# Moving the squares of x, their sum and three small loads from the first matrix product to the second

## The chip, the core and the metric

The kernel runs on one core of one Trainium2 chip. A core has five engines with queues of their own: TensorE (PE in the profile; its weight loads are listed apart as PEld), VectorE (DVE), ScalarE (ACT), GpSimd (POOL) and SyncE (SP), which here only issues DMAs. Each engine works through its own queue in order and waits on semaphores for the others. The metric is the device time of one execution in microseconds (us), lower is better.

## The reference

One layer of a decoder trunk in float32: 256 tokens, width 2048. Shortened to what matters here:

```python
h = rms_norm(x, norm_mix_pre)                 # x * rsqrt(mean(x*x) + eps) * gain
c_q, c_kv, k_r, q_s, k_s, v_s, gates = split(h @ w_in)
o_a = mla_attention(...)                      # from c_q, c_kv, k_r
o_b = swa_attention(q_s, k_s, v_s, swa_sinks, rel_bias_table)   # window of 128, bias by distance, sinks
merged = sigmoid(gA) * (o_a @ w_o_mla) + sigmoid(gB) * (o_b @ w_o_swa)
x = x + rms_norm(merged @ w_out, norm_mix_post)
x = x + rms_norm(conv_ffn(rms_norm(x, norm_ffn_pre)), norm_ffn_post)
```

The part that the change touches is the first norm, x * rsqrt(mean(x*x) + eps), and the start of the window branch (q_s, k_s, v_s).

## The kernel before

**Products.** All matrix products are done in parts: each float32 operand is split into a rounded high part and the rest, and three matmuls (high by high, high by low, low by high) make one product (`mm3`, L147 to L149). The activations are split into `ahl` (L207 on ScalarE, L208 on VectorE). Weights come in chunks of 512 KB, 128 x 1024: SyncE issues the load into one of three buffers `raw` (L119), ScalarE rounds it to `whi` (L121), VectorE takes the difference `wlo` (L122), and a ring of five `whi`/`wlo` buffers lies between these and TensorE. A `raw` buffer is given back when `wlo` is made, so the load of a chunk waits for the `wlo` of the chunk three before it.

**Products in order.** `gemm` runs over 16 blocks of 128 rows of the weights, for two blocks of 128 tokens. With 512 columns a chunk holds two blocks of rows, 12 matmuls. The first product makes the keys and values of the window branch (`acc_kv`). In it, chunks are 1, 1, 1, 1, 1, 1, 2, 2, 2, 2, 2 blocks (`XCUT`), because x itself is loaded and split beside the weights (`x_cols`, called once for each chunk). The second to fifth products make the queries of the window branch, 512 columns each; the accumulators of the third take the two PSUM buffers that `acc_kv` had.

**The norm.** The products take x times the gain, without the factor of the norm, which is applied to their results. `x_square(i)` squares part i of x on ScalarE (L246 for the first two parts, L249 after) and adds it to `sq_sum` on VectorE (L250). Of the eleven parts, 0 to 5 are squared in the first product and 6 to 10 in the second. `x_norm` adds the two halves of `sq_sum` (L280), sums over partitions with four small matmuls into `ssx` (L283), and makes the factor `r1` in some twelve small steps on VectorE.

**Steps.** Outside of the first product, work is hung on a list of steps. `at(t, f)` registers f for step t; `gemm` calls `tick()` after each chunk, which runs what is registered for that step. So step t of the second product comes behind its chunk t, counted from 0, and steps 8 to 15 belong to the third product. Before, step 3 has `swa_begin` (the norm) and `x_strip`; step 4 `swa_kv`, which reads `acc_kv` out, multiplied by `r1` (`kd` L315 and L316, `vs` L318); steps 5 to 8 have `swa_v` and `swa_k`, which flip values and keys on TensorE (`vr` L324, `kt` L331) and split the results (L204, L205). The window branch follows: transposed queries (`xp`, L369) at steps 9 and 10, the first scores (L399, L401) at step 10 with their read-out on VectorE (L403 to L405), which adds `bias`.

**The biases.** `x_strip` makes a strip of the biases with two matmuls from `relx` and `sel` (L275), copies it (L276) and writes it to memory from GpSimd's queue (L277). From there GpSimd loads `bias` for each pair of heads (L391, L392), for the first one at step 9. `sink` is used after the scores (L410).

**Order.** In the first product the order on VectorE, ScalarE and SyncE is the order of the program (`manual_schedule`, closed by `head.close()`). Behind it a scheduler sets the order on each engine, by priority and by its own estimate of when inputs are ready; the priority follows the order in which the program registers the work, `high_priority(300)` around the norm and the read-out of `acc_kv` raises theirs, and `keep_in_program_order` holds an instruction behind those that stand before it on its engine.

Of the kernel before, what the change touches and what calls it, by code (L numbers as in the profile page):

```python
# [16 lines left out]
ALU = mybir.AluOpType  # L17
AX = mybir.AxisListType

P = 128  # L20
# [21 lines left out]
def trunk_layer(ctx, tc, x, x_cols_in, conv_cols_in, g_mix_post, g_ffn_post, w_in, w_q, w_kv,  # L42
                sinks, rel, wo_a, wo_b, w_out, w_up, w_down, rope_tab, strip_sel, out):
    nc = tc.nc
    vec, act, pe, pool = nc.vector, nc.scalar, nc.tensor, nc.gpsimd
# [13 lines left out]
    def sb(pl, shape, name, dt=F32, tag=None, bufs=None):  # L59
        return pl.tile(shape, dt, name=name, tag=tag or name, **({"bufs": bufs} if bufs else {}))  # L60
# [30 lines left out]
    sink = sb(base, [P, SH], "sink")  # L91
# [37 lines left out]
    def at(t, *fs):  # L129
        steps[max(t, now[0])].extend(fs)  # L130
# [48 lines left out]
    def rsqrt(v, n, name, pl):  # L179
        y = sb(pl, [P, n], f"{name}_y")  # L180
        t = sb(pl, [P, n], f"{name}_t")
        u = sb(pl, [P, n], f"{name}_u")
        vec.tensor_scalar(y.bitcast(I32), v.bitcast(I32), -0.5, float(0x5F3759DF), op0=ALU.mult, op1=ALU.add)
        def vyy():
            if n == 1:
                vec.scalar_tensor_tensor(t, v, y[:, 0:1], y, op0=ALU.mult, op1=ALU.mult)
            else:
                vec.tensor_tensor(t, y, y, op=ALU.mult)
                vec.tensor_tensor(t, t, v, op=ALU.mult)


        vyy()
        vec.tensor_scalar(t, t, -0.5, 1.5, op0=ALU.mult, op1=ALU.add)
        vec.tensor_tensor(y, y, t, op=ALU.mult)
        vyy()
        vec.tensor_scalar(u, t, 0.375, -1.25, op0=ALU.mult, op1=ALU.add)
        vec.tensor_tensor(u, u, t, op=ALU.mult)
        vec.scalar_tensor_tensor(y, u, 1.875, y, op0=ALU.add, op1=ALU.mult)
        return y

    def split_to(hi, lo, src, scale=None):

        if scale is None:
            act.copy(hi, src)  # L204
            vec.tensor_tensor(lo, src, hi.bitcast(F32), op=ALU.subtract)  # L205
        else:
            act.activation(hi, src, AF.Copy, scale=scale)  # L207
            vec.scalar_tensor_tensor(lo, src, scale, hi.bitcast(F32), op0=ALU.mult, op1=ALU.subtract)  # L208
# [8 lines left out]
    def load_xt(i):  # L217
        k, ke = XCUT[i], XCUT[i + 1]
        if i == 0:
            nc.sync.dma_start(gx, x_cols_in[:, 0:38 + 256])  # L220
        else:
            nc.sync.dma_start(xr[i - 1], x_cols_in[:, 38 + k * 256:38 + ke * 256].rearrange("p (k n) -> p k n", n=256))
# [10 lines left out]
    sq_sum = sb(p0, [P, 2, 256], "sq_sum")  # L233
# [6 lines left out]
    def x_square(i):  # L240

        k, n = XCUT[i], XCUT[i + 1] - XCUT[i]
        src = xr[i - 1] if i else gx[:, 38:].unsqueeze(1)
        dst = sq_sum[:, k % 2:k % 2 + n, :]
        if k < 2:
            act.activation(dst, src, AF.Square)  # L246
        else:
            sq = sb(p0, [P, n, 256], f"sq{i}", tag="sq", bufs=2)
            act.activation(sq, src, AF.Square)  # L249
            vec.tensor_tensor(dst, dst, sq, op=ALU.add)  # L250

    def x_cols(k, ke):
        i = XCUT.index(k)
        if i > 0:
            load_xt(i)
        if i == X_AT:
            nc.sync.dma_start(relx[0:32, :], rel)
            nc.sync.dma_start(sel, strip_sel)
            nc.sync.dma_start(sink, sinks.partition_broadcast(P))
        if i > 7:  # L260
            x_square(2 * i - 16)
            x_square(2 * i - 15)
        for j in range(k, ke):
            src = xr[i - 1][:, j - k, :] if i else gx[:, 38:]
            split_to(XH(j), XL(j), src, gx[:, j:j + 1])
# [3 lines left out]
    relx = sb(lpool, [33, SH], "relx")  # L269
    pool.memset(relx[32:33, :], 1.0)  # L270
    sel = sb(lpool, [33, 384], "sel")

    def x_strip():
        pp = pss.tile([P, 512], F32, name="pstrip", tag="s")
        pe.matmul(pp[0:SH, 0:384], relx, sel, start=True, stop=True)  # L275
        vec.tensor_copy(sel[0:SH, :], pp[0:SH, 0:384])  # L276
        pool.dma_start(strip, sel[0:SH, :])  # L277

    def x_norm():
        vec.tensor_tensor(sq_sum[:, 0, :], sq_sum[:, 0, :], sq_sum[:, 1, :], op=ALU.add)  # L280
        pv_ = pss.tile([P, 512], F32, name="ssx", tag="s")
        for t in range(NT):
            pe.matmul(pv_[:, t:t + 1], sq_sum[:, 0, t * P:(t + 1) * P], ones, start=True, stop=True)  # L283
        vec.tensor_scalar(v1, pv_[:, 0:NT], 1.0 / D, EPS, op0=ALU.mult, op1=ALU.add)
        r = rsqrt(v1, NT, "r1", base)
        vec.tensor_scalar(r1s, r, 0.125, None, op0=ALU.mult)
        vec.tensor_scalar(rh, r, 0.5, None, op0=ALU.mult)
        return r

    warm_up(WARM[1])  # L290
    acc_kv, _ = gemm(XH, XL, w_in, 0, KT, C_KS, 512, pre=x_cols, extra={i: (None, p0, 4) for i in range(4)})
    pool.tensor_copy(gmat, gx[:, 0:38])
    head.close()
# [5 lines left out]
    def swa_begin():  # L299
        nonlocal es1, p1, r1  # L300
        with tc.high_priority(300):
            r1 = x_norm()
        es0.close()
        es1, p1 = open_pool("p1")
        kx.extend(sb(p1, [P, 2, 384], f"kx{g}", F32R) for g in range(4))
        vx.extend(sb(p1, [P, 4, 2, 64], f"vx{t}", F32R) for t in range(NT))

    def swa_kv(t):
        with tc.high_priority(300):
            swa_evac(t)  # L310

    def swa_evac(t):
        kk = sb(p1, [P, 4, 2, 64], f"kd{t}", tag="pth", bufs=2)
        a3 = acc_kv[t].rearrange("p (a b) -> p a b", b=64)
        act.activation(kk[:, :, 0, :], a3[:, 0:4, :], AF.Copy, scale=r1[:, t:t + 1])  # L315
        vec.tensor_scalar(kk[:, :, 1, :], a3[:, 0:4, :], r1[:, t:t + 1], None, op0=ALU.mult)  # L316
        v_ = sb(p1, [P, 256], f"vs{t}", tag="p", bufs=3)
        act.activation(v_, acc_kv[t][:, 256:512], AF.Copy, scale=r1[:, t:t + 1])  # L318
        kd.append(kk)
        vs.append(v_)  # L320

    def swa_v(t):
        pv_ = pss.tile([P, 512], F32, name=f"vr{t}", tag="s")
        pe.matmul(pv_[:, 0:256], flip, vs[t], start=True, stop=True)  # L324
        o = pv_[:, 0:256].rearrange("p (a b) -> p a b", b=64)
        split_to(vx[t][:, :, 0, :], vx[t][:, :, 1, :], o)

    def swa_k(g):
        pt = pst.tile([P, 512], F32, name=f"kt{g}", tag="t")
        for j, t in enumerate((1, 0, 1)):  # L330
            pe.matmul(pt[:, j * P:(j + 1) * P], kd[t][:, g, :, :].rearrange("p a b -> p (a b)"), flip, start=True, stop=True)  # L331
        split_to(kx[g][:, 1, :], kx[g][:, 0, :], pt[:, 0:384])

    now[0] = 0
    steps.clear()
    for i in range(6, len(XCUT) - 1):
        at((i - 6) // 2, lambda i=i: x_square(i))
    at(3, swa_begin, x_strip)
    for t in range(NT):
        at(4, lambda t=t: swa_kv(t))  # L340
        at(5 + t, lambda t=t: swa_v(t))
    for g in range(4):
        at(5 + g, lambda g=g: swa_k(g))
    at(18, lambda: tc.keep_in_program_order(nc.sync.dma_start(rtab, rope_tab.rearrange("(t p) a b -> p t a b", p=P))))
    at(20, lambda: tc.keep_in_program_order(nc.sync.dma_start(cvT, conv_cols_in)))

# [372 lines left out]
    for j in range(4):  # L719
        acc, _ = gemm(XH, XL, w_in, 0, KT, C_GA + 512 * j, 512)  # L720
        for t in range(NT):
            g = stg(f"ta{j}_{t}")
# [308 lines left out]

RING = 5
XCUT = [0, 1, 2, 3, 4, 5, 6, 8, 10, 12, 14, 16]
X_AT = 9
WARM = (12, 15)
EXTRA = 3
LINE_A = 80
# [67 lines left out]
```

## Time and profile before

| | |
|---|---|
| median of 3 runs | 1495.74 us (1493.18 to 1497.47) |
| profiled execution | 1493.93 us |
| its span, first to last instruction | 1492.1 us |
| granted TensorE clock | 0.998 |

In the rows of the profile stand the engine, the line of the kernel, the operation, what is written and read, and shapes. In the order in time, the first two numbers of a row are the start (us from the start of the span) and the duration, "x2" says that two instructions are merged into one row, and square brackets at the end hold how long the engine was idle before and who released it. In the list of waits stand the total, the number of times and the longest. In the rows by stretch of time stand, behind the stretch and its length, the busy time and number of instructions of PE, PEld, DVE, ACT and POOL, then the granted clock, the busy share of the DMA engines and GB/s. In the chain of waits a row has start, duration and what the end of the program hung on at that time.

### The profile page before, as it was taken

Reading aid. Unit: us, or ns where it says so; the run is one execution under the profiler, and the core shown is the slowest. Engines: PE = TensorE matmul, PEld = TensorE weight load, DVE = VectorE, ACT = ScalarE, POOL = GpSimd, SP = SyncE. Lnnn points to the kernel's source line nnn. Section 1 sums busy time; section 2 is a strip of 40 time slices with the busy share of each in tenths; the row PEclk is TensorE's granted clock in tenths of the full one; section 3 lists DMA queues with packets and bytes.
Section 4 is the critical chain, followed back from the end, with each engine's and each line's share of the span. In section 5 each row is a group of like instructions: output and inputs, shape, how many; then the busy total and the mean of one; then the engine's idle time right before and its main releaser. Section 6 shows DMA issues by size and latency. Waiting matters only on the chain.

```text
span 1492.1 us, 21213 instructions
## 1 busy us (share of the span) xinstructions
PE 1476.4 (99%) x7797; PEld 1260.5 (84%) x7797; DVE 982.5 (66%) x1720; ACT 808.7 (54%) x1336; POOL 57.1 (4%) x97
## 2 busy tenths in 40 slices
PE   8999999999999999999999999999999999999997
PEld 7888888888899988888888888888888888888887
DVE  7688884445677664655798777675444677677555
ACT  7588874434565554444666555554444555555442
POOL 0122200000000000000000000000000000000000
PEclk9999999999999999999999999999999999999999
DMA  8776566666655559765655666665666666666653
GB/s 264 207 191 172 145 181 196 203 210 208 184 156 156 171 160 320 243 213 193 196 180 173 198 184 186 188 190 187 195 194 190 188 190 185 185 186 189 191 195 114
DMA packets 162500, 285.52 MB, mean 191 GB/s; under 512 B 18603, under 2 KB 35148, under 8 KB 162268
## 3 DMA queue, kind: packets, MB, share of 16 engines
q1 hardware_dynamic: 157612, 268.39, 58.7%
q0 software_dynamic: 4784, 15.78, 4.2%
q8 instruction: 61, 1.00, 0.3%
q14 instruction: 43, 0.35, 0.1%
HBM read 277.79 MB, written 6.34 MB: 190 GB/s over the span
## 4 chain that ended last, share of the span: by engine, by line
PE 91%; DVE 4%; DMA 2%; ACT 2%; issue 1%; SPq 0%; DVEq 0%; ACTq 0%
PE accg L147 17%; PE accg L149 17%; PE accg L148 17%; PE ub L945 10%; PE ua L945 10%; PE ua L946 5%; PE ub L946 5%; DMA raw<-in_w_in_dram 2%; DVE wlo L122 1%; PE mpo L695 1%; PE ms L661 1%; ACT p L421 1%; ACT whi L121 1%; PE qn L624 1%; PE qn L625 1%
## 5 line engine op out<-in xcount | busy, mean ns | idle before, releaser
L122 DVE TENSOR_TENSOR wlo<-raw,whi 128x1024 fp32r<-128x1024 f32 (+2 forms) x503 | 609.0, 1212 | 447.6 <-ACT whi L121 447.1
L121 ACT CAST whi<-raw 128x1024 fp32r<-128x1024 f32 (+2 forms) x503 | 523.3, 1041 | 577.7 <-PE accg L149 318.7
L147 PE MATMUL accg<-whi,ahl 128*128 128x512 f32 (+1 forms) x608 | 238.5, 392 | 0.0
L148 PE MATMUL accg<-wlo,ahl 128*128 128x512 f32 (+1 forms) x608 | 236.1, 388 | 0.4 <-DVE wlo L122 0.4
L149 PE MATMUL accg<-whi,ahl 128*128 128x512 f32 (+1 forms) x608 | 235.8, 388 | 0.0
L147 PE MATMUL accg<-whi,bhl 128*128 128x512 f32 (+1 forms) x608 | 230.9, 380 | 0.0
L149 PE MATMUL accg<-whi,bhl 128*128 128x512 f32 (+1 forms) x608 | 230.1, 378 | 0.0
L148 PE MATMUL accg<-wlo,bhl 128*128 128x512 f32 (+1 forms) x608 | 230.0, 378 | 0.0
L945 PE MATMUL ua<-ahl,whi 128*128 128x512 f32 x640 | 227.1, 398 | 0.0
L945 PE MATMUL ub<-ahl,whi 128*128 128x512 f32 x640 | 226.7, 398 | 0.0
L946 PE MATMUL ua<-ahl,wlo 128*128 128x256 f32 x640 | 178.2, 281 | 0.0
L946 PE MATMUL ub<-ahl,wlo 128*128 128x256 f32 x640 | 177.9, 281 | 0.0
L945 PEld LDWEIGHTS ub<-ahl,whi 128*128 128x128 f32 x640 | 120.3, 188 | 28.8
L945 PEld LDWEIGHTS ua<-ahl,whi 128*128 128x128 f32 x640 | 120.3, 188 | 28.7
L149 PEld LDWEIGHTS accg<-whi,ahl 128*128 128x128 f32 x608 | 114.5, 188 | 23.0
L149 PEld LDWEIGHTS accg<-whi,bhl 128*128 128x128 f32 x608 | 114.4, 188 | 21.4
L147 PEld LDWEIGHTS accg<-whi,ahl 128*128 128x128 f32 x608 | 114.7, 189 | 21.0 <-ACT vs L318 0.6
L148 PEld LDWEIGHTS accg<-wlo,ahl 128*128 128x128 f32 x608 | 114.5, 188 | 21.2 <-DVE wlo L122 1.0
L148 PEld LDWEIGHTS accg<-wlo,bhl 128*128 128x128 f32 x608 | 114.4, 188 | 20.9
L147 PEld LDWEIGHTS accg<-whi,bhl 128*128 128x128 f32 x608 | 114.4, 188 | 20.7
L946 PEld LDWEIGHTS ub<-ahl,wlo 128*128 128x128 f32 x640 | 120.9, 189 | 1.0
L946 PEld LDWEIGHTS ua<-ahl,wlo 128*128 128x128 f32 x640 | 120.9, 189 | 0.9
(317 smaller groups left out, 1514.9 us busy)
## 6 DMA issues: line engine op xcount, KB each, us to landing
raw<-in_ffn_w_up_dram SPq DMA_DIRECT2D x176, 512.0 KB, 3.7
raw<-in_w_in_dram SPq DMA_DIRECT2D x109, 512.0 KB, 4.4
raw<-in_ffn_w_down_dram SPq DMA_DIRECT2D x88, 512.0 KB, 3.7
raw<-in_w_o_swa_dram SPq DMA_DIRECT2D x32, 512.0 KB, 3.9
raw<-in_w_o_mla_dram SPq DMA_DIRECT2D x32, 512.0 KB, 4.9
raw<-in_w_out_dram SPq DMA_DIRECT2D x32, 512.0 KB, 4.2
raw<-in_mla_w_q_up_dram SPq DMA_DIRECT2D x48, 128.0 KB, 2.7
bias<-strip POOLq DMA_DIRECT2D x16, 256.0 KB, 4.1
```

The costliest lines, as they stand in the source:

```text
L121: act.copy(hi[:, :n], raw[:, :n])
L122: vec.tensor_tensor(lo[:, :n], raw[:, :n], hi[:, :n].bitcast(F32), op=ALU.subtract)
L147: pe.matmul(o, ah, bh, start=start, stop=False)
L148: pe.matmul(o, ah, bl, start=False, stop=False)
L149: pe.matmul(o, al, bh, start=False, stop=stop)
L421: act.activation(pb[:, i, a:b], pb[:, i, a:b], AF.Exp, bias=st["nm"][:, i, t:t + 1], accum_out=st["sm"][:, i, t:t + 1])
L624: pe.matmul(o, wh, ch(k), start=k == 0, stop=False)
L625: pe.matmul(o, wh, cl(k), start=False, stop=False)
L661: pe.matmul(o, w, v_, start=n == 0, stop=False)
L695: pe.matmul(o, w(t), p_[:, c], start=n == 0, stop=n == 5)
L945: both = lambda: pe.matmul(o3, hi[:, c], h3[:, :, s_], start=k == 0, stop=k == KT - 1)
L946: high = lambda: pe.matmul(acc[i][:, 0:256], lo[:, c], hn[p][:, s_], start=False, stop=False)
```

## The change

All eleven squares run in the second product, two at each of the steps 0 to 4 and the last at step 5; the sum of the two halves (L280) leaves `x_norm` and gets a place of its own at step 5. The norm and the strip move from step 3 to step 6, the read-out of `acc_kv` from 4 to 7, the flips of the values from 5 and 6 to 8 and 9, those of the keys from 5, 6, 7, 8 to 8, 9, 11, 12. The loads of `relx`, `sel` and `sink` leave the first product and are issued at step 2, in program order on SyncE.

```diff
@@ x_cols
-        if i == X_AT:
-            nc.sync.dma_start(relx[0:32, :], rel)
-            nc.sync.dma_start(sel, strip_sel)
-            nc.sync.dma_start(sink, sinks.partition_broadcast(P))
-        if i > 7:
-            x_square(2 * i - 16)
-            x_square(2 * i - 15)
@@
+    def strip_loads():
+        for o, i in ((relx[0:32, :], rel), (sel, strip_sel), (sink, sinks.partition_broadcast(P))):
+            tc.keep_in_program_order(nc.sync.dma_start(o, i))
@@ x_norm
-        vec.tensor_tensor(sq_sum[:, 0, :], sq_sum[:, 0, :], sq_sum[:, 1, :], op=ALU.add)
@@
-    for i in range(6, len(XCUT) - 1):
-        at((i - 6) // 2, lambda i=i: x_square(i))
-    at(3, swa_begin, x_strip)
+    for i, t in enumerate((0, 0, 1, 1, 2, 2, 3, 3, 4, 4, 5)):
+        at(t, lambda i=i: x_square(i))
+    at(2, strip_loads)
+    at(5, lambda: vec.tensor_tensor(sq_sum[:, 0, :], sq_sum[:, 0, :], sq_sum[:, 1, :], op=ALU.add))
+    at(6, swa_begin, x_strip)
     for t in range(NT):
-        at(4, lambda t=t: swa_kv(t))
-        at(5 + t, lambda t=t: swa_v(t))
-    for g in range(4):
-        at(5 + g, lambda g=g: swa_k(g))
+        at(7, lambda t=t: swa_kv(t))
+        at(8 + t, lambda t=t: swa_v(t))
+    for g, t in enumerate((8, 9, 11, 12)):
+        at(t, lambda g=g: swa_k(g))
@@
-X_AT = 9
```

## The prediction

> **What bounds the kernel now.** I read the page's first lines, then who TensorE waited for over the whole program, then the order in time of the first 60 us, where every edited line runs.
>
> ```profile
> span 1492.1 us, 21213 instructions
> PE 1476.4 (99%) x7797; PEld 1260.5 (84%) x7797; DVE 982.5 (66%) x1720; ACT 808.7 (54%) x1336; POOL 57.1 (4%) x97
> ```
>
> ```profile
> PE warm L75 <- DVE ident_b L70: 2.1, 1, 2.1
> PE ssx L283 <- DVE sq_sum L280: 1.6, 1, 1.6
> PE ckT L499 <- DVE ckl L208: 1.3, 1, 1.3
> PE accg L148 <- DVE wlo L122: 0.4, 1, 0.4
> PE xp L369 <- ACT x L372: 0.3, 2, 0.2
> ```
>
> TensorE (PE) bounds it: busy 99% of the span, and the five largest waits of the whole program add up to 5.7 us. The first is the start, the third lies at the end of the window branch, far behind the edits. So the only wait of size that the edit touches is the second, 1.6 us for the sum of squares. It is worth reading closely.
>
> ```profile
> 28.87 0.39 PE L147 MATMUL accg<-whi,ahl 128*128 128x512 f32 x1
> 33.18 0.39 PE L148 MATMUL accg<-wlo,ahl 128*128 128x512 f32 x1
> 32.40 1.05 ACT L121 CAST whi<-raw 128x1024 fp32r<-128x1024 f32 x1 [1.24 <-DMA raw<-in_w_in_dram]
> 33.48 1.23 DVE L122 TENSOR_TENSOR wlo<-raw,whi 128x1024 fp32r<-128x1024 f32 x1 [0.99 <-ACT whi L121]
> 34.62 0.42 DVE L280 TENSOR_TENSOR sq_sum<-sq_sum 128x256 f32<-128x256 f32 x1
> 35.19 0.58 PE L283 MATMUL ssx<-ones,sq_sum 128*128 128x1 f32 x4 [1.62 <-DVE sq_sum L280]
> 35.62 0.47 PE L149 MATMUL accg<-whi,ahl 128*128 128x512 f32 x1
> ```
>
> 28.87 is the first matmul of the second product, 33.18 its twentieth: (33.18 - 28.87) / 19 = 0.227 us each, so 12 matmuls, one step of the list of steps, take 2.72 us. The norm is registered at step 3, which would be behind 48 matmuls; it stands behind 20. The high priority pulled it forward to where the scheduler thought the sum ready. On the chip the sum (L280) stood in VectorE's queue behind the weight split of the fourth chunk, that behind its rounding on ScalarE, and that behind its transfer, which landed late. From 33.41, when the next matmul was due, to 35.62 TensorE lost 2.21 us, of which 0.43 (35.62 - 35.19) are the small matmuls themselves.
>
> **The change, part by part.** First, what leaves the first product.
>
> ```profile
> 12.93 1.05 ACT L121 CAST whi<-raw 128x1024 fp32r<-128x1024 f32 x1 [0.66 <-DVE ahl L208]
> 13.10 0.56 SPq L257 DMA_DIRECT2D relx<-in_rel_bias_table_dram  x1
> 14.15 0.36 SPq L259 DMA_DIRECT2D sink<-in_swa_sinks_dram  x1
> 15.29 0.50 PE L148 MATMUL accg<-wlo,ahl 128*128 128x512 f32 x1 [0.38 <-DVE wlo L122]
> 16.23 0.41 ACT L246 ACTIVATE sq_sum<-gx 128x256 f32<-128x256 f32 x1
> 19.28 0.72 ACT L249 ACTIVATE sq<-xr 128x256 f32<-128x256 f32 x2
> 21.64 0.72 ACT L249 ACTIVATE sq<-xr 128x256 f32<-128x256 f32 x2
> 20.55 0.76 DVE L250 TENSOR_TENSOR sq_sum<-sq_sum,sq 128x256 f32<-128x256 f32 x2
> 23.14 0.75 DVE L250 TENSOR_TENSOR sq_sum<-sq_sum,sq 128x256 f32<-128x256 f32 x2
> ```
>
> Six squares leave ScalarE, two of 0.41 and two pairs of 0.72, together 2.26 us; four additions leave VectorE, 0.76 + 0.75 = 1.51 us; three small loads leave SyncE's queue, 13.10 to 14.51. But TensorE's only wait in this product, 0.38 us at 15.29, goes back to a rounding at 12.93, ahead of the first small load and of the first square. Later the helpers are full and TensorE doesn't feel it:
>
> ```profile
> 20.00:25.00 5.00, 5.00 (x23) 4.11 (x22) 5.00 (x11) 5.00 (x10) 0.00 (x0) 1.00 0.67 195
> 30.00:35.00 5.00, 3.57 (x16) 2.63 (x14) 4.00 (x5) 3.25 (x4) 0.00 (x0) 1.00 0.85 265
> 35.00:40.00 5.00, 4.82 (x23) 4.10 (x24) 4.23 (x16) 1.44 (x2) 0.00 (x0) 1.00 0.80 235
> ```
>
> Between 20 and 25, VectorE and ScalarE are busy 5.00 of 5.00, and so is TensorE. So the first product gains nothing: **0**, bounds -0.4 (that wait gone) to 0.
>
> Second, the same 2.26 and 1.51 us come into the second product, beside five squares that are there already. ScalarE has room (3.25 and 1.44 of 5 in the two later stretches), VectorE less (4.00 and 4.23). They cost TensorE nothing themselves, hidden by weights that are split ahead of use; without that cover they would cost 1.51. They act through the sum, **the wait at ssx**. Best case it is gone, -1.6; worst, the 1.51 us of additions all land ahead of L280 and TensorE comes no later, +1.5. The chunk ahead of L280 was split at 34.71, and unstalled matmuls would need it at 28.87 + 3 x 2.72 = 37.03, a lead of 2.3 us. Three chunks on:
>
> ```profile
> 39.62 1.05 ACT L121 CAST whi<-raw 128x1024 fp32r<-128x1024 f32 x1 [2.17 <-PE accg L149]
> ```
>
> There ScalarE waits for TensorE to give back a buffer, not for a transfer: the lead has filled the ring. A sum asked for three steps later is asked for where the helpers are that far ahead. Also, additions that sit in VectorE's full stretch at 20 to 25 no longer delay the weights of the chunks behind. I take a wait of 0.4 where 1.6 is now: **-1.2**.
>
> Third, the small loads.
>
> ```profile
> 12.16 6.05 DMA raw<-in_w_in_dram
> 27.59 4.73 DMA raw<-in_w_in_dram
> raw<-in_w_in_dram SPq DMA_DIRECT2D x109, 512.0 KB, 4.4
> ```
>
> The weight transfer issued just ahead of them took 6.05 us, the median of its kind 4.4: at worst they delay a neighbour by 1.65. In the new place, behind the third chunk's issue, their 1.41 us of issue time fills about the gap to the next issue (27.59). The fourth chunk is again the neighbour, but the sum is no longer behind it. **0**, bounds 0 to +1.65. The Trainium skill, DMA: Bandwidth & Descriptors, section Specifications, says that a transfer needs pieces of 512 B or more to run at line rate; rows of relx and sink hold 32 numbers, 128 B, so by it this cost is theirs and moves with them. The 6.05 agrees, though a chunk of x was in flight as well.
>
> Fourth, the products that flip values and keys (vr, kt) and their splits move behind steps 8 to 12, beside the first transposes and scores of the window branch, which use the same two-buffer PSUM pools.
>
> ```profile
> 42.19 0.83 PE L275 MATMUL pstrip<-sel,relx 33*32 33x384 f32 x2
> 42.36 0.87 ACT L318 ACTIVATE vs<-accg,r_y 128x256 f32<-128x256 f32 x2
> 44.61 0.67 POOL L277 DMA_DIRECT2D strip<-sel  x1 [41.11 <-DVE sel L276]
> 48.99 0.75 POOL L391 DMA_DIRECT2D bias<-strip  x1 [3.71 <-PE accg L149]
> 51.34 0.55 DVE L205 TENSOR_TENSOR kx<-kt,kx 128x384 fp32r<-128x384 f32 x1
> 56.29 0.83 PE L331 MATMUL kt<-flip,kd 128*128 128x128 f32 x6
> 56.88 0.48 PE L147 MATMUL accg<-whi,ahl 128*128 128x512 f32 x1
> 67.11 0.29 DVE L403 TENSOR_TENSOR p<-s,bias 128x128 f32<-128x128 f32 x1 [1.49 <-PE s L401]
> DMA to landing us min/median/max: 3.6/5.4/6.5
> 62.00:97.00 35.00, 34.78 (x190) 29.34 (x189) 28.31 (x88) 25.57 (x62) 7.35 (x10) 1.00 0.71 179
> ```
>
> Six hand-overs, each waiting at worst for one split of 0.55: 0 to +3.3. The nearest rows, waits of transposes in that branch, are 0.3 in two: **+0.3**.
>
> Fifth, what is hidden. The accumulators of keys and values are read out by 42.36 + 0.87 = 43.23, 8.0 us behind ssx, and wanted again by the third product at 56.88: 13.6 us to spare. Three steps take 8.2 of it, and two vr and three kt groups that no longer stand ahead, at most 0.59 each (56.88 - 56.29), take 3.0: 2.4 left, **0**. The strip of biases: pstrip at 42.19 + 8.2 - 1.2 = 49.2; the second load of unit 0 is issued 6.80 + 0.75 later (as 48.99 stands to 42.19) and lands within 6.5: 63.2. L403 reads it, now at 67.11, then 1.2 earlier and without two kt groups of 0.59 ahead: 64.7. It is 1.5 us in time: **0**. If not, VectorE stands at L403 with the weight splits of later chunks queued behind it.
>
> **Sum:** 0 - 1.2 + 0 + 0.3 + 0 = -0.9. The profiled execution took 1493.93, so 1493.0; the median shown, 1495.74, is 1.81 above it, so 1494.8.
>
> **The rivals.** *The wait travels along.* The scheduler puts the norm where it thinks the sum ready, as it does now, and errs by as much: 1.6 stays, 0.3 is added: 1496.0. For it: the norm's present place, two steps ahead of its step. Against: the grown lead. If the scheduler pulls squares and norm so far forward that the order hardly changes, the time is the same.
>
> *The small loads' neighbour.* They delay the fourth chunk by 1.65, and the sum, further down the same queue, gains as much less: 1494.8 + 1.65 = 1496.5. For it: the 6.05; against: the 4.73 at 27.59, with no small load near, is slow too. This is the rule of the page DMA: Bandwidth & Descriptors in the Trainium skill, weighed above.
>
> *Slower: VectorE falls behind at the start of the window branch.* The key and value splits, six of up to 0.55 = 3.3 us, arrive together with the first scores, and L403 behind them. It decides from the point where bias or splits come later than 64.7, 1.5 us from the sum above, and more than the split weights cover. Price 3.3 with no gain at ssx: 1495.74 + 3.3 = 1499.0. For it: the 1.5 us are short. Against: VectorE is busy only 28.31 of 35.00 between 62 and 97.
>
> **How the numbers follow.** Forecast 0.45, wait travels 0.25, small loads 0.10, slower 0.20. Predicted 1494.8. The shown runs lie 2.6 below to 1.7 above their median. Low: both touched waits gone, 1495.74 - 1.6 - 0.4 - 2.6 = 1491.1; high: 1499.0 + 1.7 = 1500.7. Range 1491.0 to 1500.7; the likeliest alone 1492.5 to 1497. A difference under 0.3%, 4.5 us, is about what a measurement of this kernel can't tell from none. Faster than that needs more than all of TensorE's waits behind the start (5.7 - 2.1 = 3.6): 0.07, out of the forecast's tail. Slower than that is the upper half of the slower rival, 0.10, and 0.04 of the others: 0.14. Within: 0.79.
>
> **What would show it.** Right: TensorE's wait at ssx under 0.8, standing around the fourth or fifth chunk of the second product; the first product's last matmul still near 28.6; no wait of TensorE over 0.5 between 45 and 80. Wrong: a wait at ssx of 1.5 or more; L403 waiting for bias; a wait of the third product's first matmul for the read-out of keys and values; new waits at kt, xp or s.

## The result, and the profile after

| | before | after |
|---|---|---|
| median of 9 runs each, us | 1495.74 | 1499.16 |
| lowest to highest, us | 1492.43 to 1497.47 | 1498.03 to 1500.5 |
| profiled execution, us (span) | 1493.93 (1492.1) | 1500.5 (1498.7) |

The changed kernel takes 1.0029 of the time before, 95% interval 1.0021 to 1.0038: 3.4 us slower by the medians. The two profiled executions differ by 6.6 us, since the one of before is a short run and the one of after the longest of its nine. Where the time went is read from that pair; how much it is, from the medians.

The page's first lines and TensorE's three longest waits, in the kernel after:

```profile
span 1498.7 us, 21206 instructions
PE 1476.4 (99%) x7797; PEld 1261.0 (84%) x7797; DVE 982.4 (66%) x1720; ACT 807.8 (54%) x1336; POOL 57.0 (4%) x97
```

```profile
PE warm L75 <- DVE ident_b L70: 8.9, 1, 8.9
PE ssx L279 <- DVE sq_sum L335: 1.9, 1, 1.9
PE ckT L497 <- DVE ckl L208: 1.2, 1, 1.2
```

The work of each engine is the same as before to 1 us. What has grown is the first wait, 2.1 before and 8.9 now: the start. The wait at ssx, which the forecast wanted at 0.4, is still there, 1.9. Next come picked rows of the timeline of the first 14 us of the kernel after (start, duration, engine and line; in brackets the idle time ahead and what ended it):

```profile
2.91 0.42 ACT L246 ACTIVATE sq_sum<-gx 128x256 f32<-128x256 f32 x1 [0.89 <-DMA gx<-in_x_cols_dram]
4.44 0.42 ACT L246 ACTIVATE sq_sum<-xr 128x256 f32<-128x256 f32 x1 [1.11 <-DMA xr<-in_x_cols_dram]
6.59 0.42 ACT L249 ACTIVATE sq<-xr 128x256 f32<-128x256 f32 x1 [1.74 <-DMA xr<-in_x_cols_dram]
7.04 0.43 DVE L250 TENSOR_TENSOR sq_sum<-sq_sum,sq 128x256 f32<-128x256 f32 x1 [7.04 <-ACT sq L249]
7.71 0.42 ACT L249 ACTIVATE sq<-xr 128x256 f32<-128x256 f32 x1 [0.70 <-DMA xr<-in_x_cols_dram]
8.16 0.42 DVE L250 TENSOR_TENSOR sq_sum<-sq_sum,sq 128x256 f32<-128x256 f32 x1 [0.69 <-ACT sq L249]
8.63 0.22 DVE L70 CAST ident_b<-ident 128x128 bf16<-128x128 f32 x1
8.91 3.06 PE L75 MATMUL warm<-ident_b 128*128 128x128 bf16 x27 [8.91 <-DVE ident_b L70]
9.04 0.42 ACT L249 ACTIVATE sq<-xr 128x256 f32<-128x256 f32 x1 [0.92 <-DMA xr<-in_x_cols_dram]
9.86 0.60 ACT L121 CAST whi<-raw 128x512 fp32r<-128x512 f32 x1
...
11.73 0.62 PE L147 MATMUL accg<-whi,ahl 128*128 128x512 f32 x1
...
13.34 0.39 PE L147 MATMUL accg<-whi,ahl 128*128 128x512 f32 x1
```

The squares, registered for the second product, are the first things that ScalarE and VectorE do at all. Each waits for its part of x to land (the last of these at 9.04), and behind them in the same queues stand ident_b, which the warm-up matmuls read, and the first rounding of a weight. The cast of ident_b, which let the warm-up begin at 2.08 before, comes at 8.63 (the Trainium skill, TensorE: Matmul & The Clock Gate, the table at its head, says that ScalarE and VectorE work their queues strictly in order; this row agrees). The first matmul of the first product, at 4.90 before, comes at 11.73, right behind the warm-up, 2.82 us after its start as before (4.90 - 2.08); its weight was rounded by 9.86 + 0.60 = 10.46.

The queues of the two kernels as they were built show that this order was built in and is no accident of the run. The head of ScalarE's queue in the kernel after ("+": not there before):

```
+L246 Activation sq_sum<-gx 128x256
+L246 Activation sq_sum<-xr_118 128x256
+L249 Activation sq_424<-xr_119 128x256
+L249 Activation sq_427<-xr_120 128x256
+L249 Activation sq_448<-xr_121 128x256
 L226 TensorCopy first<-ident 128x1
 L207 Activation ahl_133<-gx 128x256
```

The rest of the first product, around the norm: picked rows of the timeline, and then two windows (length, busy time and count of PE, PEld, DVE, ACT, POOL, granted clock, DMA share, GB/s) of the kernel after:

```profile
28.67 2.35 DVE L122 TENSOR_TENSOR wlo<-raw,whi 128x1024 fp32r<-128x1024 f32 x2
...
29.89 0.39 PE L148 MATMUL accg<-wlo,ahl 128*128 128x512 f32 x1
...
30.94 0.68 DVE L250 TENSOR_TENSOR sq_sum<-sq_sum,sq 128x512 f32<-128x512 f32 x1
31.65 0.42 DVE L335 TENSOR_TENSOR sq_sum<-sq_sum 128x256 f32<-128x256 f32 x1
32.22 0.72 PE L279 MATMUL ssx<-ones,sq_sum 128*128 128x1 f32 x4 [1.95 <-DVE sq_sum L335]
32.81 0.77 PE L149 MATMUL accg<-whi,ahl 128*128 128x512 f32 x1
...
35.94 0.39 PE L147 MATMUL accg<-whi,ahl 128*128 128x512 f32 x1
...
37.99 0.39 PE L147 MATMUL accg<-whi,ahl 128*128 128x512 f32 x1
```

```profile
32.50:35.90 3.40, 3.40 (x10) 2.77 (x10) 3.08 (x11) 1.05 (x1) 0.00 (x0) 0.50 0.71 207
35.90:37.00 1.10, 1.10 (x6) 0.89 (x5) 0.71 (x5) 0.00 (x0) 0.00 (x0) 0.99 1.02 374
```

Not one square is left in the second product: the last addition starts at 30.94, and the second product's first matmul, the 97th, is the one at 37.99. The norm came forward as well. Its small matmuls stand behind 80 matmuls of the first product instead of behind 20 of the second, and wait there for a sum that stands, as before, behind weight splits on VectorE (28.67, 2.35 us for two). And when TensorE goes on, the granted clock is 0.50 for 3.4 us: the seven matmuls from 32.81 to 35.94 take 3.13 us where seven take 7 x 0.227 = 1.59.

The account of the pair, at the 97th matmul (28.87 before, 37.99 after):

| part | us |
|---|---|
| first matmul 11.73 for 4.90 | +6.83 |
| first six matmuls 1.61 (11.73 to 13.34) for 2.75 (4.90 to 7.65) | -1.14 |
| wait at 15.29 before, 0.38 and its restart, gone | -0.54 |
| loss at ssx, now ahead of this point: next matmul due at 30.12, comes at 32.81 | +2.69 |
| half clock behind it, 3.13 for 1.59 | +1.54 |
| small gaps | -0.26 |
| 97th matmul | +9.12 |
| loss at ssx of before, which comes behind this point | -2.21 |
| small gaps of both, behind it | -0.3 |
| profiled execution | +6.6 |

The second row is a gift of the late start, and in part luck of the pair. Before, the matmuls are 0.43 apart until 7.65 and 0.23 from there; after, they are 0.23 apart from 12.18 on. The rows by stretch show a granted clock of 1.00 for both starts, but the trace's own record of the clock begins, with full clock, at 7.64 before and at 12.03 after. In the runs below whose first matmul also comes at 4.90 to 5.07, it begins between 5.10 (e8) and 8.09 (e9), so another execution of before could have lost less here. Behind the window branch nothing changes: the offset of the same weight's rounding is 6.7 us at 296 us (302.84 for 296.12) and 6.7 us at 1469 (1475.41 for 1468.71).

### The profile page after: what moved, and what is told of

Same layout as the page of the kernel before. It is cut to its first block, busy times and chain, and to the rows that moved or that the text cites. A ratio compares the mean times of both kernels' runs of the same rounds, so it can differ in the third digit from the quotient of the medians.

```text
span 1498.7 us, 21206 instructions
## 1 busy us (share of the span) xinstructions
PE 1476.4 (99%) x7797; PEld 1261.0 (84%) x7797; DVE 982.4 (66%) x1720; ACT 807.8 (54%) x1336; POOL 57.0 (4%) x97
## 4 chain that ended last, share of the span: by engine, by line
PE 91%; DVE 4%; ACT 2%; DMA 2%; issue 1%; SPq 0%; DVEq 0%; ACTq 0%
PE accg L149 18%; PE accg L147 17%; PE accg L148 17%; PE ub L943 10%; PE ua L943 10%; PE ua L944 5%; PE ub L944 5%; DMA raw<-in_w_in_dram 1%; DVE wlo L122 1%; PE mpo L693 1%; PE ms L659 1%; ACT p L419 1%; ACT whi L121 1%; PE qn L622 1%; PE qn L623 1%
```

## The experiments

Two theories stood against each other. *Queue heads*: the time is lost since squares run ahead of the start, in both queues; held where the diff writes them, the change would cost little. The rival: it is lost at ssx, from the norm's and the loads' new places, or is the late warm-up alone. Each run is compared with the kernel before on the same chip; the place of ssx is counted in matmuls ahead of it.

| run | median, us (runs) | ratio to before [95%] | first matmul | TensorE's largest waits behind the start | half clock |
|---|---|---|---|---|---|
| after | 1499.16 (9) | 1.0029 [1.0021, 1.0038] | 11.73 | ssx 1.9 | 3.41 us |
| e1_held | 1497.89 (7) | 1.0026 [1.0015, 1.0037] | 5.02 | ssx 3.5 | 6.83 us |
| e2_squares | 1498.39 (10) | 1.0022 [1.0013, 1.0032] | 12.15 | ssx 0.9, ckT 0.9 | none |
| e3_rest | 1496.78 (11) | 1.0013 [1.0004, 1.0022] | 4.90 | ssx 2.7 | none |
| e4_adds_held | 1499.13 (5) | 1.0032 [1.0019, 1.0044] | 9.33 | first matmul 4.2, ssx 2.6 | 3.41 us |
| e8_loads | 1498.24 (10) | 1.0019 [1.0009, 1.0028] | 4.91 | ssx 2.6, weights 1.6 in three | 3.41 us |
| e10_head_free | 1496.60 (11) | 1.0010 [1.0001, 1.0019] | 4.90 | ssx 3.0, ckT 1.1 | 3.41 us |
| e5_before_ssx_held | 1496.38 (12) | 1.0007 [0.9999, 1.0016] | 4.90 | kt 3.0, weights 1.2 in three | none |
| e6_both_held | 1498.72 (10) | 1.0024 [1.0015, 1.0033] | 5.07 | kt 4.0 | 3.41 us |
| e7_after_ssx_held | 1503.91 (6) | 1.0057 [1.0044, 1.0071] | 12.02 | kt 3.5, ckT 2.4 | 6.83 and 3.41 us |
| e9_flips_late | 1495.45 (11) | 1.0002 [0.9993, 1.0011] | 4.90 | xp 2.1 | 3.41 us |
| e11_flips_apart | 1495.03 (11) | 1.0000 [0.9991, 1.0009] | 4.98 | xp 2.3 | none |

First matmul, waits and half clock are of each one's profiled execution, which is a single one; other runs of the same kernel can have more or fewer half clocks (see the last section).

### The squares alone, and the rest alone

e2 is the kernel before with only the squares moved; e3 is the kernel after with the squares left as before.

```diff
 # e2
-        if i > 7:
-            x_square(2 * i - 16)
-            x_square(2 * i - 15)
...
-    for i in range(6, len(XCUT) - 1):
-        at((i - 6) // 2, lambda i=i: x_square(i))
+    for i, t in enumerate((0, 0, 0, 0, 1, 1, 1, 1, 2, 2, 2)):
+        at(t, lambda i=i: x_square(i))
```

> The kernel before with only the squares moved out of the first product, free, to steps 0 to 2; small loads, norm, keys and values stay where they were. Theory: the first matmul at 11 to 12 us and 1.002 to 1.004 of before, as in the changed kernel. Rival (the three later steps or the loads): 0.999 to 1.001.

> The changed kernel with the squares left as they were before (parts 0 to 5 in the first product, 6 to 10 in the second); loads, sum, norm, keys and values at the new steps. Theory: first matmul near 4.9 us, 0.998 to 1.001 of before. Rival: 1.002 to 1.004.

In e2 the warm-up begins at 9.3 and the first matmul at 12.15. TensorE's waits in e2, and then in e3:

```profile
PE warm L75 <- DVE ident_b L70: 9.3, 1, 9.3
PE ckT L496 <- DVE ckl L208: 0.9, 1, 0.9
PE ssx L280 <- DVE sq_sum L277: 0.9, 1, 0.9
```

```profile
PE ssx L282 <- DVE sq_sum L338: 2.7, 1, 2.7
PE warm L75 <- DVE ident_b L70: 2.1, 1, 2.1
PE accg L148 <- DVE wlo L122: 0.9, 3, 0.3
```

The squares alone bring the late start and 1.0022, most of the whole. The rest alone brings no late start, a longer wait at ssx than before (2.7 for 1.6), and 1.0013, which lies between the two ranges expected. Both parts cost; e2 is the larger by its point value, though the two intervals overlap.

### The queue heads

e1 keeps all squares and additions where the diff writes them, e4 only the additions on VectorE. e10 goes the other way: the kernel after, in which a square may not be issued ahead of the rounding of the seventh weight chunk, and is free otherwise.

```diff
 # e1
+        hold = tc.keep_in_program_order
-            act.activation(dst, src, AF.Square)
+            hold(act.activation(dst, src, AF.Square))
...
-            act.activation(sq, src, AF.Square)
-            vec.tensor_tensor(dst, dst, sq, op=ALU.add)
+            hold(act.activation(sq, src, AF.Square))
+            hold(vec.tensor_tensor(dst, dst, sq, op=ALU.add))
 # e10, both squares
-            act.activation(sq, src, AF.Square)
+            with tc.issue_after(rounded[6].ins):
+                act.activation(sq, src, AF.Square)
```

> The changed kernel with every square and every addition held in program order on its engine, so that they run in the second product as the diff reads. Theory (the scheduler pulled the free squares to the heads of ScalarE's and VectorE's queues, and the identity casts and the first roundings stand behind them): the first matmul of the first product is back near 4.9 us (11.73 in the changed kernel), the time 0.997 to 1.001 of before. Rival (norm, key and value steps or the loads cost the time): first matmul near 4.9 too if the squares are held, but the ratio stays at 1.002 to 1.004, with new waits of TensorE between 30 and 80 us.

> The changed kernel with only the additions of the squares held in program order on VectorE; the squares on ScalarE are free. Theory, in two halves: VectorE's identity casts are first again, so the warm-up matmuls start near 2.1 us instead of 8.9; but the first rounding on ScalarE still stands behind the squares of parts 0 to 3, whose x lands by 7.7, so the first matmul comes at 10 to 11.7 us and the ratio is 1.001 to 1.004. If the late warm-up alone costs the time: first matmul near 5, ratio 0.998 to 1.001.

> The changed kernel with every square queued on ScalarE behind the rounding of the seventh chunk of the first product, free behind that; nothing else differs. It takes the squares from the heads of the queues and leaves the scheduler the rest. Theory: first matmul back near 4.9 us, a wait at ssx of 1.5 to 3 us stays since the scheduler still places it early, 0.9990 to 1.0015 of before, 2 to 4 us under the changed kernel. Rival (the late start costs nothing in the end): 1.0025 to 1.0035 as in the changed kernel.

TensorE's waits in e4, then picked rows of the timeline of e10:

```profile
PE accg L147 <- ACT whi L121: 4.2, 1, 4.2
PE ssx L280 <- DVE sq_sum L336: 2.6, 1, 2.6
PE warm L75 <- DVE ident_b L70: 2.1, 1, 2.1
```

```profile
2.08 3.06 PE L75 MATMUL warm<-ident_b 128*128 128x128 bf16 x27 [2.08 <-DVE ident_b L70]
...
4.90 0.78 PE L148 MATMUL accg<-whi,ahl 128*128 128x512 f32 x1
...
14.72 0.40 ACT L248 ACTIVATE sq_sum<-gx 128x256 f32<-128x256 f32 x1
...
33.46 0.58 PE L282 MATMUL ssx<-ones,sq_sum 128*128 128x1 f32 x4 [2.97 <-DVE sq_sum L338]
```

In e4 the warm-up is back at 2.1, and the first matmul comes at 9.33 all the same, for its weight waits on ScalarE (4.2). So the late warm-up isn't the whole cause: both queue heads hold the start. In the kernel after, VectorE's is the later one, since the first matmul stands right behind the warm-up there. That e4 starts 2.4 us earlier than after and is no faster has a reason in its start: its matmuls are 0.43 apart until 13.21. e10 takes the squares from both heads: first squares at 14.72, start at 4.90 as before, and the ratio falls from 1.0029 to 1.0010, by the point values 0.19%, 2.8 us; the two intervals do not overlap. That is what the late start costs, net of what else this edit changes. It is less than 6.8 since the late start brings its gifts (-1.14 and -0.54 above), and since the scheduler now puts ssx behind 102 matmuls instead of 80, where its wait has grown to 2.97, with a half clock behind it.

e1 was to be the change as its diff reads. The start is back (5.02), and still it costs 1.0026. TensorE's longest wait and the windows behind it in e1:

```profile
PE ssx L280 <- DVE sq_sum L336: 3.5, 1, 3.5
```

```profile
40.00:44.00 4.00, 0.97 (x5) 1.00 (x5) 3.37 (x4) 1.61 (x2) 0.00 (x0) 0.87 0.74 193
44.00:48.00 4.00, 4.00 (x11) 3.13 (x11) 2.41 (x10) 1.04 (x1) 0.00 (x0) 0.50 0.68 222
```

TensorE works 0.97 of the 4 us from 40 to 44, then at half clock. So the theory that only the heads matter falls too: the wait at ssx is a second cause. It is longer here, where the squares are held: the last addition comes at 41.74, behind a weight split, and the sum at 42.46.

### The small loads

e8 is the kernel before with only the three small loads moved.

```diff
-        if i == X_AT:
-            nc.sync.dma_start(relx[0:32, :], rel)
-            nc.sync.dma_start(sel, strip_sel)
-            nc.sync.dma_start(sink, sinks.partition_broadcast(P))
...
+    at(2, strip_loads)
```

> The kernel before with only the three small loads moved to step 2 of the second product. If they delay the fourth chunk and with it the sum: a wait at ssx over 2.2 us and 1.0005 to 1.0015 of before. If not: 0.9995 to 1.0005 and a wait of 1.6.

TensorE's waits in e8:

```profile
PE ssx L283 <- DVE sq_sum L280: 2.6, 1, 2.6
PE warm L75 <- DVE ident_b L70: 2.1, 1, 2.1
PE accg L148 <- DVE wlo L122: 1.6, 3, 0.7
```

A move that was priced at nothing costs 1.0019 [1.0009, 1.0028]. The trace does not put this on the loads' transfers in their new place. They are issued from 26.96 on, and the three waits for weights, 1.6 together where before has one of 0.4, stand ahead of that, at 7.53, 15.28 and 19.00; e5, which leaves the loads alone, has three as well (1.2). Nor does the sum come later: ssx runs at 34.57, before at 35.19. It is the scheduler again: the edit touches SyncE's queue alone, but ssx now stands behind 9 matmuls of the second product instead of 20, and so waits 2.6 for 1.6; a half clock follows. Why the scheduler puts it there stays open.

### Can the wait at ssx be removed?

Here the theory was that the scheduler's early placing of the norm costs 1.6 us or more that can be had back. e5 holds the small matmuls of before where they are registered; e6 does so on top of e1, e7 in the kernel after. e9 and e11 are e5 with the flips of values and keys later, held too, at different steps.

```diff
 # e5, e6, e7
-            pe.matmul(pv_[:, t:t + 1], ...)
+            tc.keep_in_program_order(pe.matmul(pv_[:, t:t + 1], ...))
 # e9, with the matmuls of vr and kt held like those of ssx; in e11 the values at 7 + t, the keys at 7, 8, 11, 12
-        at(5 + t, lambda t=t: swa_v(t))
-    for g in range(4):
-        at(5 + g, lambda g=g: swa_k(g))
+        at(8 + t, lambda t=t: swa_v(t))
+    for g, t in enumerate((8, 9, 11, 12)):
+        at(t, lambda g=g: swa_k(g))
```

> The kernel before with the four small matmuls of the norm held in program order on TensorE, so that they stand at step 3, behind 48 matmuls of the second product instead of 20. Theory (TensorE stalls because ssx stands ahead of where its sum is ready, and the runs above the lowest carry a dip of the granted clock behind that stall): no wait at ssx, no dip, 0.9975 to 0.9995 of before, and the runs within 2 us of each other. Rival (the stall only moves, to the weights or to the read-out of keys and values): 0.9995 to 1.0005.

> The changed kernel with squares and additions held in program order, as in the first run of the series, and ssx held too, so that it stands at step 6. Theory: first matmul near 5 us, the wait of 3.5 us at ssx gone, no dip: 0.9975 to 1.0000 of before, some 4 us under the run with the squares alone held. Rival (the later read-out of keys and values makes TensorE wait at the third product, or the squares slow the weights of the second): 1.0005 to 1.003.

> The changed kernel, squares free, with only ssx held at step 6. Theory (late start and stall are two separate costs): first matmul still at 11.7 us, no wait at ssx, no dip, 1.001 to 1.0025 of before, and 3 to 6 us over the kernel with both held. If the late start costs nothing, because the loads run on meanwhile and it is caught up: 0.998 to 1.000.

> The kernel before with ssx held at step 3, as in the run that held it alone, and the flips of keys and values moved to steps 8, 9, 11 and 12 as in the change and held in program order there, so that the factor of the norm has time to get through VectorE's queue. Theory (every wait of TensorE here comes from a product that the scheduler put ahead of its input, and a version without such a wait beats both kernels): no wait of TensorE over 0.5 us between 16 and 70 us but for the weights, no dip of the clock, 0.9975 to 0.9990 of before. Rival (the stall turns up again, at the third product or at the first scores): 0.9995 to 1.0010.

> The kernel before with ssx held at step 3 and the flips held at steps 7 and 8 (values) and 7, 8, 11 and 12 (keys), so that no flip shares a step with the first transposed queries of the window branch, where the run with steps 8 and 9 had a wait of 2.07 us for a PSUM buffer. Theory: no wait of TensorE over 0.6 us between 5 and 200 us, no dip of the clock, all runs within 2.5 us, 0.9980 to 0.9995 of before. Rival (a wait of 1.5 us or more turns up at another place): 0.9995 to 1.0010.

Picked rows of the timeline of e5 from ssx to the flips, and one of that of e11:

```profile
40.66 0.50 PE L283 MATMUL ssx<-ones,sq_sum 128*128 128x1 f32 x4
...
43.69 1.23 DVE L122 TENSOR_TENSOR wlo<-raw,whi 128x1024 fp32r<-128x1024 f32 x1 [0.39 <-ACT whi L121]
44.83 0.15 DVE L284 TENSOR_SCALAR v<-ssx 128x2 f32<-128x2 f32 x1
...
46.48 1.23 DVE L122 TENSOR_TENSOR wlo<-raw,whi 128x1024 fp32r<-128x1024 f32 x1 [0.36 <-ACT whi L121]
...
48.60 0.16 DVE L198 SCALAR_TENSOR_TENSOR r_y<-r_u,r_y 128x2 f32<-128x2 f32 x1
...
50.17 0.87 DVE L316 TENSOR_SCALAR kd<-accg,r_y 128x256 f32<-128x256 f32 x2
...
51.25 0.91 PE L331 MATMUL kt<-flip,kd 128*128 128x128 f32 x6 [2.98 <-issue]
```

```profile
63.17 0.54 PE L369 MATMUL xp<-ident_r,qx 128*128 128x128 f32 x4 [2.31 <-DVE kx L205]
```

ssx itself no longer waits. But from its matmuls to the root r_y pass 8 us (40.66 to 48.60), since the small steps (128x2 numbers each) stand among splits on VectorE that wait for their weights; the keys are scaled from 50.17 to 51.04, and the flip comes at 51.25 after a wait of 2.98 (the profile names no releaser for it; this row fits in time). Moved later, the flips let the next transposes (xp) wait, for the PSUM buffer that the split of the keys (L205) gives back. A wait of 2 to 4 us came back each time, at kt or at xp, and no version is shown to be faster than before: the intervals of e5, e9 and e11 hold 1. That the wait can be had back so is not borne out. e6, at 1.0024, lands in its rival's range, by a wait at kt. e7, with the late start and the late norm, is the slowest of all, 1.0057, above both of its ranges.

## Why the prediction was wrong

The forecast, 1494.8, named a small gain; the median came out 3.4 us above before, inside the range (1491.0 to 1500.7) and outside the likeliest case's own (1492.5 to 1497).

**The step that failed first** is "the same 2.26 and 1.51 us come into the second product". The prediction read the steps of the diff as places. It had seen the norm stand ahead of its step, but did not ask the same of the squares, which left a block whose order is written by hand for one that the scheduler orders. None of them runs in the second product. With it "So the first product gains nothing", with bounds of -0.4 to 0, failed: its start lost 6.83. The bound was one-sided, since a loss from work that *leaves* was not thought of. The first rival came near it: "If the scheduler pulls squares and norm so far forward that the order hardly changes, the time is the same." They were pulled forward past their old places, to the heads of the queues, and so the order did change. e2 shows this step by itself (1.0022), e10 takes it back (1.0010 left).

**The wait at ssx**, -1.2 in the sum. It stayed: 1.95 for 1.62, its loss 2.69 for 2.21; 1.5 or more was the prediction's own sign of being wrong. This is the rival "the wait travels along", and the runs speak for it wherever norm or loads move: 2.7 in e3, 2.6 in e8, 3.0 in e10, 3.5 in e1 (e2, which moves neither, has 0.9). The grown lead, on which the -1.2 rested, did not help, as the scheduler's place for the norm came forward, to where the sum stands behind weight splits on a VectorE that has no gap (24.7 to 33.2 in the kernel after).

**The half clock** behind a wait was no term at all: +1.54 in the profile of after.

**The small loads**, 0 with bounds to +1.65. The point was wrong: moved alone in e8 they cost 0.19%, 2.8 us; the interval, 0.09% to 0.28%, 1.3 to 4.2 us, still reaches below the upper bound. The step asked for the neighbour's transfer only, not for what the edit makes of the scheduler's other choices. Within the whole change the price can't be read apart.

**Right in the run of after**: the flips (+0.3), the read-out and the bias strip (0 each). Two rows of the timeline of after; L401 adds the bias, as L403 did before:

```profile
57.12 0.83 PE L272 MATMUL pstrip<-sel,relx 33*32 33x384 f32 x2
...
72.63 0.29 DVE L401 TENSOR_TENSOR p<-s,bias 128x128 f32<-128x128 f32 x1 [1.98 <-PE s L399]
```

It waited for the score, not for the bias, although pstrip came 14.9 us later than before; and TensorE has no wait over 0.3 between 45 and 80. So the slower rival, VectorE behind at the window branch, did not happen: the slowdown came by another way, and that its 1499.0 lies next to the measured 1499.16 is luck.

## What to carry to other kernels

A step that a diff moves out of a block ordered by hand into one that a scheduler orders has no fixed place: ask where it may go at the earliest, and whether it then stands, waiting for a load, at the head of a queue that the start needs. Look at the order of each queue as built before pricing a move in time. And if a wait goes back to a chain of small steps among long ones on one engine, moving its reader moves the wait; shorten the chain's place in that queue instead (this last was not tried here).

## What the runs showed of the hardware

The granted clock falls to 0.50 after some short waits of TensorE and stays there for 3.41 us, or twice that, 6.83: 1.54 us lost in the 3.41 of the kernel after. It followed waits of 1.95 (after), 2.07 (e9), 2.4 (ckT in e7), 2.6 (e4, e8), 2.97 (e10), 3.5 (e1, e7) and 4.0 (e6), and did not follow 1.62 (before), 0.9 (e2), 2.31 (e11), 2.7 (e3) and 2.98 (e5). Between 1.95 and 2.98 the length of the wait doesn't decide.

What decides, as far as these runs show, is how much of the wait falls into one stretch of a grid. In the traces' record of the clock, each time at full clock between the start and the first fall is a whole multiple of 3.413 us: 6 of them in after, 8 in e10, 9 in e8, 10 in e4, 11 in e1, 14 in e7, 15 in e6 and 16 in e9. Laid on this grid, all thirteen profiles agree: half clock follows every stretch in which TensorE is idle for 1.95 us or more, and none in which it is idle for 1.69 us or less. (This counts the four small matmuls of ssx as idle; counted as work, the stretch ahead of e4's half clock would have 1.51 and not fit. Values between 1.69 and 1.95 did not occur.) Two stretches each of e9 and of e3:

```profile
59.29:62.70 3.41, 1.34 (x13) 1.13 (x11) 2.51 (x4) 3.11 (x6) 0.00 (x0) 1.00 0.54 159
62.70:66.11 3.41, 3.41 (x13) 2.73 (x12) 1.44 (x3) 1.17 (x2) 0.00 (x0) 0.50 0.81 222
```

```profile
30.00:33.41 3.41, 1.74 (x8) 1.12 (x6) 3.04 (x5) 1.58 (x2) 0.00 (x0) 1.00 0.77 225
33.41:36.82 3.41, 2.33 (x12) 2.06 (x13) 2.55 (x7) 2.09 (x2) 0.00 (x0) 1.00 0.73 231
```

The wait of 2.07 in e9 lies in one stretch, 1.34 of 3.41 busy, and half clock follows. The longer one of e3, 2.74, is cut in two by the grid, 1.67 and 1.07, and the clock stays full.

The Trainium skill, TensorE: Matmul & The Clock Gate, Part 1 (The HAM clock gate), tells of a window of 3413 ns that runs freely, whatever the kernel does, and of half clock after an idle window. The grid of 3.413 us agrees, and so does the start, where full clock comes between 5.10 and 8.09 in runs whose first matmul comes at 4.90 to 5.07. That an idle window is one of about 3.4 us without work does not agree as it stands: 1.95 us was enough here.

The half clocks go with the spread of the runs. Of the 83 runs of before that the experiments were compared with, the 48 with a mean granted clock of 0.998 or more have a median of 1494.24 us, the 35 with less one of 1496.19. In e3, whose profile has no half clock, the four runs at 0.998 take 1494.97 to 1495.29 us and the five at 0.996 1497.62 to 1499.82. That the same waits cause it in those runs is argued only, as they have no trace.
